# Two-layer recurrent trunk on one core: the second layer's embeddings placed between two matrix products, and a seven-product scheme on two more chunks

## The chip, the core and the metric

The kernel runs on one core of a Trainium2 chip. The core has a matrix engine (TensorE, PE in the profile, with PEld for the loading of its stationary operand), three engines for elementwise work (VectorE or DVE, ScalarE or ACT, GpSimd or POOL) and SyncE (SP), whose queue here only issues transfers. Each takes its instructions in the order that was fixed when the kernel was built, and waits on semaphores. The metric is the device time of one execution in microseconds.

## The reference

The reference computes, for 256 positions of width 2048, two layers of token mixers with residual adds, each followed by a gated per-layer embedding, and a last RMS norm. What matters here is the second layer (odd: `mlstm`) and the line of the embedding:

```
u = hn @ o_w_in[j]
qk, v, og, z, ig, fg = the columns of u (2048, 2048, 2048, 2048, 8, 8)
qk = jax.nn.silu(causal_conv(qk, c_conv_w[j], c_conv_b[j]))
...
yc = mlstm(q, k, v, li, lf)
yc = head_rmsnorm(yc, c_norm[j]) * jax.nn.sigmoid(og) * jax.nn.silu(z)
h = h + yc @ o_w_out[j]
pl = rmsnorm(p[i] @ ple_w[i], ple_norm[i])
h = h + jax.nn.sigmoid(h @ ple_gate_w[i]) * pl
```

The embedding `p[i] @ ple_w[i]` (256 x 256 by 256 x 2048) depends on nothing that the layer computes. All numbers are fp32.

## The kernel before

**Products in fp32.** Every fp32 operand is split into a rounded high part and a remainder (`hi`, `lo`), and a product is three matmuls: high by high, high by low, low by high. The weights are split as they arrive: `load_weights` (L124) takes a tile of 128 x 1024 (512 KB) into the ring `raw` (5 buffers), casts it on ScalarE into `whi` (L135) and subtracts on VectorE into `wlo` (L136), 4 buffers each. The activations, 256 positions by 2048 features, lie feature-major in `act`, eight entries of two blocks of 128 features each; they are TensorE's stationary operand, and the weights stream past in 512 columns.

**Chunks and quarters.** A weight matrix of 2048 columns is four chunks of 512; a chunk is four quarters of its 2048 rows. `quarter_tok` (L185) loads a quarter (two tiles) and issues 24 matmuls: 4 blocks of rows, two halves of the positions, three matmuls each. `project_tok` (L161) does a chunk; `project_two` (L170) does chunks 0 and 1 with their last quarters at the end, so that those features of the input that come late are wanted late; `chunks` (L180) is `project_two` and then chunks one by one. The two halves of a chunk are two accumulators in PSUM, from the pool `pm` (tag mm, 3 banks) or `px` (tag mx, 3 banks).

**Seven products.** `seven` (L262) does two chunks `j` and `j + 1` together. On their first quarter (256 features) it forms a 2 x 2 scheme over halves of the positions and the two chunks, with seven block products in place of eight: sums and differences of the weights on VectorE (`add`, L276), sums of the activations prepared once for all pairs (`combos`, L231, which gives `qs`), and combinations of the results in PSUM with the saved product `p1` (`soon`, L280; the copy of `p1`, L288). The other three quarters are plain (`plain`, L223, whose matmuls are at L217). It yields four results: chunk and half (0, 0), (0, 1), (1, 0), (1, 1). Its weights X and Y lie in tiles of tag ch (`chain`, 2 buffers), W and Z in the ring; the partial results in four half tiles from two tiles of tag h (`part`). The pool `hp` has four tiles of tag h; before this stage they hold the hidden state `hq`, which is sent away to DRAM (L1070) and fetched back (L1335). `combos` holds two scratch tiles of tag hn (3 buffers) through its three steps, and a third within each.

**Order.** The code is a list of instructions, and a scheduler puts each engine's share in order by its place in the list and by when its inputs are expected. `tc.high_priority(offset=n)` counts an instruction as if it stood n places earlier: 400 for weight casts and splits, 450 for `soon` and the copy of `p1`. Side work stands in lanes, generators that `pump` (L75) steps once in the middle of each quarter; `drain` steps a lane to its end. A lane often carries data from token-major to feature-major: two transposes on VectorE, one transfer to DRAM and four back on POOL's queue (`across`, L597), some pumps of lag, then scale, cast and split (L631, L149 and L150 for the gates; L492, L149 and L150 for the first layer's gate output, which makes `act` for the second layer).

**The second layer.** Its matrix products come in this order:
- queries and keys (`oqk`, L1126): four chunks by `chunks`; each is scaled to `tqk` and goes through `features` (L1096: hop across DRAM, convolution L1118, SiLU) in a lane;
- values (`ov`, L1267): four chunks, with the gate statistics and the mixing of the heads (`mix`) in lanes; `combos` starts after chunk 2;
- output gates (`oog`, L1308): two pairs by `seven`;
- z gates (`oz`, L1318): two pairs by `seven`; the result of chunk `j` is multiplied with the mixed heads and goes through lane `fm{j}` to `y`;
- the reload of the hidden state (L1335), then the embedding (`embed`, L411, called at L1345): two weight tiles' worth of chunks b, two halves c each, two halves of the positions, each a group of 6 matmuls (L438) in a bank of `pm` of its own, copied out to `pl` by ScalarE (L450, first half) or VectorE (L448, second half); in the first layer these copies have a preference of 600, here none;
- the output projection (`oo`, L1371): `chunks`, whose quarter kq waits for `y[2 kq]` and `y[2 kq + 1]`, that is for `fm{kq}`;
- the gate of the embedding and the last norm.

Of the kernel before, what the change touches and what calls it, by code (L numbers as in the profile page):

```python
# [19 lines left out]
P = 128  # L20
# [23 lines left out]
def trunk(ctx: ExitStack, tc: tile.TileContext, a, out):  # L44
# [37 lines left out]
    def drain(*which):  # L82
        for lane in which:
            while step(lane):
                pass
# [325 lines left out]
    def embed(w, pact, tile_of, first=None):  # L411

        pls = []
        for b in range(2):
            head = first and b == 0
            if head:
                part, pact = load_head(w[0])
                parts = [part] + load_weights(w[0], (1, 2), (1,))
            else:
                parts = load_weights(w[b], *(((2, 1),) if first else ()))  # L420
            if first and b:
                first()
            for c, (hi, lo) in enumerate(parts):
                terms = [(hf, k, x, y, 0, 512) for hf in range(2) for k in range(2) for x, y in ((0, 0), (0, 1), (1, 0))]
                if head:
                    terms.sort(key=(lambda t: (t[3], t[3] and t[0], t[1])) if c == 0 else
                               (lambda t: (t[1], t[3] if t[1] == 0 else t[0], t[3])))
                    if c == 0:
                        terms[0:4] = [(hf, 0, x, 0, o, T) for o in (0, T) for x in range(2) for hf in range(2)]
                pool, name = (px, "mx") if first and c == 0 else (pm, "mm")  # L430
                ps = [pool.tile([P, 512], F32, name=name, tag=name) for _ in range(2)]
                halves = []
                for n, (hf, k, x, y, o, w_) in enumerate(terms):
                    mine = [m for m, t in enumerate(terms) if t[0] == hf]
                    with ExitStack() as behind:
                        if first and "pe" in last:
                            behind.enter_context(tc.issue_after(last["pe"]))
                        last["pe"] = te.matmul(ps[hf][:, o:o + w_], tokens(pact[x], k, hf),  # L438
                                               (hi, lo)[y][:, k * 512 + o:k * 512 + o + w_],
                                               start=(n == mine[0]), stop=(n == mine[-1])).ins  # L440
                    if n < mine[-1]:
                        continue
                    pl = tile_of()
                    with ExitStack() as order:
                        if first:
                            order.enter_context(tc.high_priority(offset=600))
                        if hf and (b or not first):
                            v.tensor_copy(pl, ps[hf])  # L448
                        else:
                            s.copy(pl, ps[hf])  # L450
                    halves.append(pl)
                pls.append(halves)
        return pls
# [639 lines left out]
    with tc.tile_pool(name="m1", bufs=2) as m1:  # L1093
# [41 lines left out]
        VW = 258  # L1135
        vts = []
# [129 lines left out]
        qs = {}  # L1266
# [23 lines left out]
        turn = []  # L1290

        def part():
            n = len(turn) % 4
            turn.append(n)
            return store_of[n // 2][:, n % 2 * 512:(n % 2 + 1) * 512]

        def chain():
            return m1.tile([P, 1024], F32, name="ch", tag="ch", bufs=2)

        def pair(w, jj):  # L1300
            return seven(w, jj, acth, qs, chain, part)

        def mixed_gates():
            for j, th in [x for x in held if x[0] in nums]:
                v.scalar_tensor_tensor(nums[j], th, 1.0, nums[j], op0=ALU.add, op1=ALU.mult)
            held[:] = [x for x in held if x[0] not in nums]

        for jj in (0, 2):  # L1308
            ths = [m1.tile([P, 2, 512], F32, name="tho", tag="vt", bufs=6) for _ in range(2)]
            for b, hf, src in pair(a["oog"], jj):  # L1310
                s.activation(ths[b][:, hf], src, AF.Tanh, scale=norm["rth"][:, hf:hf + 1])
                if hf:
                    held.append((jj + b, ths[b]))
                    if jj + b == 3:
                        drain("mix")
                    mixed_gates()
        pact = load_p()
        for jj in (0, 2):  # L1318
            us = [m1.tile([P, 2, 512], F32, name="u", tag="vt", bufs=6) for _ in range(2)]
            for b, hf, src in pair(a["oz"], jj):  # L1320
                j, u = jj + b, us[b]
                with tc.high_priority(offset=100):
                    s.activation(u[:, hf], src, AF.Tanh, scale=norm["rth"][:, hf:hf + 1])
                    v.scalar_tensor_tensor(u[:, hf], u[:, hf], 1.0, src, op0=ALU.add, op1=ALU.mult)
                for i in range(2):
                    c = hf * 8 + 2 * j + i
                    e = slice(i * 256, (i + 1) * 256)
                    v.scalar_tensor_tensor(u[:, hf, e], u[:, hf, e], fac[:, c:c + 1], nums[j][:, hf, e],
                                           op0=ALU.mult, op1=ALU.mult)
                if hf:  # L1330
                    start(f"fm{j}", feature_major(u, "cn", 4 * j, y, 5))
# [3 lines left out]
            gp.dma_start(out=t, in_=away[c])  # L1335
            hq.append(t)

        pairs = []

        def pl_half():  # L1340
            n = len(pairs)
            pairs.append(pairs[n - 2] if n % 4 > 1 else m1.tile([P, 1024], F32, name="pl", tag="qk", bufs=4))
            return pairs[n][:, n % 4 // 2 * 512:(n % 4 // 2 + 1) * 512]
# [244 lines left out]
```

## Time and profile before

| | |
|---|---|
| median of 3 runs | 1034.44 us (1032.46 to 1036.43) |
| the profiled execution | 1034.75 us, span 1033.0 us |
| mean granted TensorE clock | 0.996 |
| DMA | 239.00 MB, mean 231 GB/s |

The span runs from the first to the last instruction of the profiled execution; the rest of its time lies around it. In the profile's rows by line, "mean ns of one" for matmuls is their modelled duration, and neighbours overlap; their pace is read from the distance of their starts. In rows of the timeline the first number is the start, the second the length, both in microseconds; what stands in brackets is the idle time of the engine just before and what ended it. In rows of stretches (start:end, length) the values are the busy time of PE, PEld, DVE, ACT and POOL with their instructions in parentheses, then the granted clock, the share of the DMA engines, and GB/s. In rows of the chain of waits: start, length, what.

The second layer's stages in this execution, from the same rows: queries and keys from about 475, values from about 563, output gates from 661.8, z gates to 833.6, the embedding from 833.62 to 849.67, then the output projection.

### The profile page before, as it was taken

The numbers are of one execution on the slowest core, as the hardware profiler recorded it, in microseconds if no ns is written. First come the engines' busy times: TensorE is split into PE (matmuls) and PEld (weight loads), VectorE is DVE, ScalarE is ACT, GpSimd is POOL, SyncE is SP. The second block draws the span as 40 slices with busy tenths as digits, with TensorE's granted clock in tenths as the row PEclk, the third lists the DMA queues.
The fourth block names the chain that finished last, engine by engine and source line by source line (L and its number), as shares of the span: only waits on it lengthen the run. The fifth ranks groups of instructions, "written<-read, shape, count | busy, mean of one in ns | idle before, by whom it ended". The sixth has DMA issues, their size and how long they took to land.

```text
span 1033.0 us, 14470 instructions
## 1 busy us (share of the span) xinstructions
PE 1020.5 (99%) x5206; PEld 847.1 (82%) x5206; DVE 786.8 (76%) x1194; ACT 615.8 (60%) x883; POOL 95.0 (9%) x178
## 2 busy tenths in 40 slices
PE   9999999999999999999999999999999989999996
PEld 8888888888888888887888888888888878888886
DVE  7858968969685776767569987887788886766684
ACT  7675545586964444565557876765565576344562
POOL 0111101011111111111021000000001111111000
PEclk9999999999999999999999999999999999999999
DMA  9987756567788897798797755464666787788652
GB/s 361 332 246 229 222 164 204 187 197 241 225 255 294 274 267 249 235 293 269 231 292 230 220 178 168 154 202 160 210 205 229 238 286 264 215 290 272 200 185 82
DMA packets 68808, 239.00 MB, mean 231 GB/s; under 512 B 8928, under 2 KB 10336, under 8 KB 68736
## 3 DMA queue, kind: packets, MB, share of 16 engines
q1 hardware_dynamic: 55584, 196.51, 58.4%
q0 software_dynamic: 12720, 41.04, 13.2%
q8 instruction: 41, 0.67, 0.3%
q10 hardware_dynamic: 432, 0.52, 0.1%
q14 instruction: 31, 0.25, 0.1%
HBM read 218.11 MB, written 19.92 MB: 230 GB/s over the span
## 4 chain that ended last, share of the span: by engine, by line
PE 93%; DMA 2%; issue 2%; ACT 1%; POOL 1%; DVE 0%; ACTq 0%; POOLq 0%
PE mm L196 21%; PE mm L197 21%; PE mm L198 21%; PE mm L217 9%; PE mx L196 4%; PE mx L197 4%; PE mx L198 4%; PE mx L217 3%; DMA r<-ducn 1%; PE mm L438 1%; PE nu L1241 1%; PE mm L1414 1%; PE mm L1413 1%; PE mm L1412 1%; DMA ducn<-w 1%
## 5 line engine op out<-in xcount | busy, mean ns | idle before, releaser
L136 DVE TENSOR_TENSOR wlo<-raw,whi 128x1024 fp32r<-128x1024 f32 (+1 forms) x341 | 411.8, 1215 | 168.3 <-ACT whi L135 158.6
L135 ACT CAST whi<-raw 128x1024 fp32r<-128x1024 f32 (+1 forms) x341 | 356.0, 1048 | 279.8 <-PE mm L198 184.0
L196 PE MATMUL mm<-whi,ahl 128*128 128x512 f32 x960 | 375.1, 391 | 0.0
L197 PE MATMUL mm<-wlo,ahl 128*128 128x512 f32 x960 | 373.9, 389 | 0.0
L198 PE MATMUL mm<-whi,ahl 128*128 128x512 f32 x960 | 373.6, 389 | 0.0
L196 PEld LDWEIGHTS mm<-whi,ahl 128*128 128x128 f32 x960 | 180.2, 188 | 38.2 <-issue 0.8
L198 PEld LDWEIGHTS mm<-whi,ahl 128*128 128x128 f32 x960 | 180.2, 188 | 37.7
L197 PEld LDWEIGHTS mm<-wlo,ahl 128*128 128x128 f32 x960 | 180.2, 188 | 37.0 <-DVE wlo L136 0.5
L217 PE MATMUL mm<-whi,ahl 128*128 128x512 f32 x320 | 101.2, 389 | 0.0
L217 PEld LDWEIGHTS mm<-whi,ahl 128*128 128x128 f32 x320 | 60.1, 188 | 12.4
L196 PE MATMUL mx<-whi,ahl 128*128 128x512 f32 x160 | 62.2, 389 | 0.0
L197 PE MATMUL mx<-wlo,ahl 128*128 128x512 f32 x160 | 62.2, 389 | 0.0
L198 PE MATMUL mx<-whi,ahl 128*128 128x512 f32 x160 | 62.2, 389 | 0.0
L217 PE MATMUL mm<-wlo,ahl 128*128 128x512 f32 x160 | 62.2, 389 | 0.0
L217 PE MATMUL mx<-whi,ahl 128*128 128x512 f32 x112 | 37.2, 390 | 0.0
L217 PEld LDWEIGHTS mm<-wlo,ahl 128*128 128x128 f32 x160 | 30.0, 188 | 6.3
L198 PEld LDWEIGHTS mx<-whi,ahl 128*128 128x128 f32 x160 | 30.0, 188 | 6.3
L196 PEld LDWEIGHTS mx<-whi,ahl 128*128 128x128 f32 x160 | 30.0, 188 | 6.2
L197 PEld LDWEIGHTS mx<-wlo,ahl 128*128 128x128 f32 x160 | 30.0, 188 | 6.2
L207 DVE TENSOR_TENSOR wlo<-ch,whi 128x1024 fp32r<-128x1024 f32 x20 | 24.1, 1222 | 9.6 <-ACT whi L206 8.9
L206 ACT CAST whi<-ch 128x1024 fp32r<-128x1024 f32 x20 | 21.0, 1051 | 13.1 <-PE mm L217 12.1
L217 PEld LDWEIGHTS mx<-whi,ahl 128*128 128x128 f32 x112 | 21.0, 188 | 4.3
(368 smaller groups left out, 1093.6 us busy)
## 6 DMA issues: line engine op xcount, KB each, us to landing
raw<-in_ew_dram SPq DMA_DIRECT2D x64, 512.0 KB, 5.0
raw<-in_g_dram SPq DMA_DIRECT2D x64, 512.0 KB, 4.9
raw<-in_eo_dram SPq DMA_DIRECT2D x32, 512.0 KB, 5.8
raw<-in_oqk_dram SPq DMA_DIRECT2D x32, 512.0 KB, 4.9
raw<-in_ov_dram SPq DMA_DIRECT2D x32, 512.0 KB, 4.2
raw<-in_oo_dram SPq DMA_DIRECT2D x32, 512.0 KB, 4.9
raw<-in_oog_dram SPq DMA_DIRECT2D x28, 512.0 KB, 4.1
raw<-in_oz_dram SPq DMA_DIRECT2D x28, 512.0 KB, 4.4
```

The source lines that it names most:

```text
L135: last["act"] = s.copy(h, r).ins
L136: last["dve"] = v.tensor_tensor(out=l, in0=r, in1=h.bitcast(F32), op=ALU.subtract).ins
L196: te.matmul(ps[hf], xh, wh, start=(k == 0), stop=False)
L197: te.matmul(ps[hf], xh, wl, start=False, stop=False)
L198: last["pe"] = te.matmul(ps[hf], xl, wh, start=False, stop=(k == KT - 1)).ins
L206: last["act"] = s.copy(hi, r).ins
L207: last["dve"] = v.tensor_tensor(out=lo, in0=r, in1=hi.bitcast(F32), op=ALU.subtract).ins
L217: last["pe"] = te.matmul(o, x, y, start=(first and k + i == 0), stop=(end and k == n - 1 and i == 2), skip_group_check=True).ins
L438: last["pe"] = te.matmul(ps[hf][:, o:o + w_], tokens(pact[x], k, hf), (hi, lo)[y][:, k * 512 + o:k * 512 + o + w_], start=(n == mine[0]), ...
L1241: te.matmul(ps[:, 0:n], x[:, i, o:o + P], y[:, b, i], start=(b == 0 and x is sh and y is vh), stop=(b == hf and y is vl))
L1412: te.matmul(o, xh, wh, start=(k == 0), stop=False)
L1413: te.matmul(o, xh, wl, start=False, stop=False)
```

## The change

Three things are changed.

1. The copies of the second layer's embedding out of PSUM get a preference of 450 instead of none.
2. Chunks 2 and 3 of the queries and keys are computed by `seven` instead of chunk by chunk. So `combos` starts before the queries and keys and steps in the pumps of their first quarters, and what `pair` needs (`part`, `chain`) is set up there; chunks 0 and 1 stay with `project_two`.
3. The embedding is called between the two pairs of z chunks instead of after both; its tiles and their loads from memory come with it.

```diff
@@ embed
-                        if first:
-                            order.enter_context(tc.high_priority(offset=600))
+                        order.enter_context(tc.high_priority(offset=600 if first else 450))
@@ queries and keys
-        for j, ps in enumerate(chunks(a["oqk"], 4, acth, ready(acth, "fg"))):
+        qs = {}
+        start("combos", combos(acth, 0, qs))
+        tqk = {}
+
+        def queries(j, hf, src):
+            if hf == 0:
+                tqk[j] = m1.tile([P, 2, 512], F32, name="tqk", tag="vt", bufs=6)
+            s.activation(tqk[j][:, hf], src, AF.Copy, scale=norm["rt"][:, hf:hf + 1])
+            if hf:
+                start(f"qk{j}", features(tqk[j], j))
+                step(f"qk{j}")
+
+        for j, ps in enumerate(project_two(a["oqk"], acth, ready(acth, "fg"))):
             if j == 0:
                 drain("norm")
-            t = m1.tile([P, 2, 512], F32, name="tqk", tag="vt", bufs=6)
             for hf in range(2):
-                s.activation(t[:, hf], ps[hf], AF.Copy, scale=norm["rt"][:, hf:hf + 1])
-            start(f"qk{j}", features(t, j))
-            step(f"qk{j}")
+                queries(j, hf, ps[hf])
+
+        drain("combos")
+        store_of = [hp.tile([P, 1024], F32, name="pr", tag="h") for _ in range(2)]
...
+        def pair(w, jj):
+            return seven(w, jj, acth, qs, chain, part)
+
+        for b, hf, src in pair(a["oqk"], 2):
+            queries(2 + b, hf, src)
@@ values
-            if j == 2:
-                start("combos", combos(acth, 0, qs))
...
-        drain("combos")
-        store_of = [hp.tile([P, 1024], F32, name="pr", tag="h") for _ in range(2)]
...
@@ z gates
         pact = load_p()
         for jj in (0, 2):
+            if jj:
+                pls = embed(a["pw1"], pact, pl_half)
             us = [m1.tile([P, 2, 512], F32, name="u", tag="vt", bufs=6) for _ in range(2)]
...
-        pls = embed(a["pw1"], pact, pl_half)
```

More of the change, by code (lines that the diff above doesn't have):

```diff
@@ L1124, in features, with part, chain @@
                 yield
-        for j, ps in enumerate(chunks(a["oqk"], 4, acth, ready(acth, "fg"))):
+        qs = {}
[9 more added lines that the diff above has]
+        for j, ps in enumerate(project_two(a["oqk"], acth, ready(acth, "fg"))):
             if j == 0:
                 drain("norm")
-            t = m1.tile([P, 2, 512], F32, name="tqk", tag="vt", bufs=6)
             for hf in range(2):
-                s.activation(t[:, hf], ps[hf], AF.Copy, scale=norm["rt"][:, hf:hf + 1])
-            start(f"qk{j}", features(t, j))
-            step(f"qk{j}")
+                queries(j, hf, ps[hf])
+        drain("combos")
+        store_of = [hp.tile([P, 1024], F32, name="pr", tag="h") for _ in range(2)]
+        turn = []
+        def part():
+            n = len(turn) % 4
+            turn.append(n)
+            return store_of[n // 2][:, n % 2 * 512:(n % 2 + 1) * 512]
+        def chain():
+            return m1.tile([P, 1024], F32, name="ch", tag="ch", bufs=2)
+        def pair(w, jj):
+            return seven(w, jj, acth, qs, chain, part)
+        for b, hf, src in pair(a["oqk"], 2):
+            queries(2 + b, hf, src)
         VW = 258
@@ L1264, in mix_norm @@
             yield
-        qs = {}
         for j in range(4):
@@ L1287, in trunk @@
         held = []
-        drain("combos")
-        store_of = [hp.tile([P, 1024], F32, name="pr", tag="h") for _ in range(2)]
[L1290 to L1301, printed above, removed]
         def mixed_gates():
@@ L1316, in trunk, with pl_half @@
                     mixed_gates()
+        pairs = []
+        def pl_half():
+            n = len(pairs)
+            pairs.append(pairs[n - 2] if n % 4 > 1 else m1.tile([P, 1024], F32, name="pl", tag="qk", bufs=4))
+            return pairs[n][:, n % 4 // 2 * 512:(n % 4 // 2 + 1) * 512]
         pact = load_p()
         for jj in (0, 2):
+            if jj:
+                pls = embed(a["pw1"], pact, pl_half)
             us = [m1.tile([P, 2, 512], F32, name="u", tag="vt", bufs=6) for _ in range(2)]
@@ L1336, in trunk @@
             hq.append(t)
[L1338 to L1343, printed above, removed]
-        pls = embed(a["pw1"], pact, pl_half)
         pss = m1.tile([P, 4, 2], F32, name="pss", bufs=1)
```

## The prediction

> **What bounds the kernel now.** I read the page's totals first, then TensorE's waits, then the chain of waits in order of time for TensorE's pace.
>
> ```profile
> span 1033.0 us, 14470 instructions
> PE 1020.5 (99%) x5206; PEld 847.1 (82%) x5206; DVE 786.8 (76%) x1194; ACT 615.8 (60%) x883; POOL 95.0 (9%) x178
> ...
> PE mm L438 <- ACT pl L450: 1.8, 1, 1.8
> PE mm L438 <- DVE pr L280: 1.2, 1, 1.2
> PE st L97 <- PEq L1579: 0.8, 1, 0.8
> PE mx L438 <- ACT whi L407: 0.3, 1, 0.3
> ...
> 510.53 1.00 PE mx L1062 x16
> ...
> 712.75 2.72 PE mx L217 x12
> ...
> 733.15 21.76 PE mm L217 x96
> 754.91 2.72 PE mx L217 x12
> ```
>
> TensorE is busy for 99% of the span. Between the start and the tail only two waits stand, both at L438 behind copies out of PSUM; they fall at 837 and 842, in the second layer's embed. So a saving must be fewer matmuls or a smoother embed; nothing else on TensorE can be won. The pace: 96 matmuls in 21.76 us are 0.227 us each (the "mean ns of one", 389, overlaps its neighbour). The two mx rows mark the same point of two neighbouring pairs: 42.16 us, which is 186 matmuls; two chunks the plain way (2 x 4 quarters x 24) are 192, or 43.5 us, 5.44 us a quarter.
>
> ```profile
> 833.62 0.39 PE L438 MATMUL mm<-whi,ahl 128*128 128x512 f32 x1
> ...
> 836.12 0.39 PE L438 MATMUL mm<-whi,ahl 128*128 128x512 f32 x1
> 836.36 0.57 ACT L450 COPY pl<-mm 128x512 f32<-128x512 f32 x1
> 836.87 0.68 DVE L280 TENSOR_TENSOR pr<-mm,pr 128x512 f32<-128x512 f32 x1
> ...
> 837.70 0.47 PE L438 MATMUL mm<-whi,ahl 128*128 128x512 f32 x1 [1.19 <-DVE pr L280]
> ...
> 840.09 0.51 ACT L631 ACTIVATE xr<-r,prm 128x256 f32<-128x256 f32 x1 [1.78 <-DMA r<-ducn]
> 840.31 0.39 PE L438 MATMUL mm<-whi,ahl 128*128 128x512 f32 x1
> ...
> 841.85 0.56 ACT L450 COPY pl<-mm 128x512 f32<-128x512 f32 x1
> ...
> 842.46 0.50 PE L438 MATMUL mm<-whi,ahl 128*128 128x512 f32 x1 [1.76 <-ACT pl L450]
> ...
> 849.67 0.39 PE L196 MATMUL mm<-whi,ahl 128*128 128x512 f32 x1
> ...
> 842.40:847.20 4.80, 4.74 (x14) 3.76 (x15) 3.85 (x7) 3.38 (x8) 0.00 (x0) 0.64 0.85 317
> ```
>
> The 48 matmuls of this embed run from 833.62 to 849.67, 16.05 us where 48 x 0.227 = 10.88 would do: 5.17 lost. From start to start less one matmul, the first gap is 837.70 - 836.12 - 0.23 = 1.35 (the third PSUM bank was still to be read by the pair's last combination, L280), the second 842.46 - 840.31 - 0.23 = 1.92. In the second, ScalarE had stood 1.78 us at the front of its queue for the hop of chunk 2's gates (r<-ducn) and took other work before the copy at 841.85. What remains, 5.17 - 1.35 - 1.92 = 1.90, is slow matmuls: in the last row the granted clock is 0.64 for 4.8 us, which alone is (1 - 0.64) x 4.8 = 1.7.
>
> **The change, part by part.**
>
> (1) Seven products for chunks 2 and 3 of queries and keys: 192 matmuls become 186, **-1.36 us** on the path. DMA stays at 16 tiles of 512 KB. Beside TensorE it adds three splits (19 for 16), four sums of weights, six combinations (24 of L280 in four pairs) and one copy:
>
> ```profile
> L136 DVE TENSOR_TENSOR wlo<-raw,whi 128x1024 fp32r<-128x1024 f32 x337 | 409.1, 1221 | 167.8 <-ACT whi L135 158.2
> L280 DVE TENSOR_TENSOR pr<-mm,pr 128x512 f32<-128x512 f32 x20 | 13.6, 682 | 0.0
> L276 DVE TENSOR_TENSOR ch<-ch,raw 128x1024 f32<-128x1024 f32 x8 | 9.8, 1222 | 0.1
> L135 ACT CAST whi<-raw 128x1024 fp32r<-128x1024 f32 x337 | 353.6, 1053 | 279.3 <-PE mm L198 184.0 <-PE mx L198 45.6 <-PE mm L217 15.8
> ...
> 519.70:563.20 43.50, 43.50 (x194) 36.02 (x193) 34.55 (x51) 27.97 (x41) 7.83 (x16) 1.00 0.86 266
> 563.20:606.70 43.50, 43.50 (x200) 36.18 (x199) 42.53 (x75) 32.97 (x52) 2.90 (x6) 1.00 0.70 215
> 606.70:661.80 55.10, 55.10 (x282) 47.16 (x281) 41.26 (x66) 38.54 (x83) 0.11 (x1) 1.00 0.46 148
> 791.60:833.60 42.00, 42.00 (x187) 34.78 (x186) 38.20 (x47) 26.73 (x35) 6.84 (x13) 1.00 0.77 251
> ```
>
> VectorE: 3 x 1.22 + 4 x 1.22 + 6 x 0.68 = 12.6 us; ScalarE: 3 x 1.05 + 0.57 (a copy as at 836.36) = 3.7. In the rows by stage the fourth value is VectorE's busy time. Chunks 2 and 3 ran from 519.7 to 563.2 with 34.55 of it; with 12.6 more it is 47.2 in 42.2, so 5.0 us too much, and the next stage (42.53 of 43.5) has 1.0 free. The rest must slip past 606.7, where 55.1 - 41.26 leaves 13.8, and the moved combos 4.9 more. What slips should be the convolutions and gate statistics, which have no preference, while splits and sums have 400 and combinations 450; the last gates' pair ran 38.20 of 42.0 without a TensorE wait. Cost on the path: from 0 (no TensorE wait stands there that could be won) to 5.0; I take 0.
>
> The first product needs a weight tile of tag ch at 519.7 (511.53, the end of L1062, plus 36 matmuls), the second 1.4 us later.
>
> ```profile
> 511.64 0.80 SPq L268 DMA_DIRECT2D ch<-in_oog_dram  x2
> ...
> DMA to landing us min/median/max: 4.2/4.9/7.0
> ```
>
> These loads, then for the next matrix, started just as L1062 ended. With the same start X lands at 515.8 to 518.6 and is split 2.3 us later, 518.1 to 520.9: 0 to 1.0 late; I take **+0.2**.
>
> (2) Combos, twelve VectorE and four ScalarE instructions, go from the values' stage to the first quarters of queries and keys. They hold all three buffers of tag hn (a21, a11 and the third), which the features of gate chunks 2 and 3 use too.
>
> ```profile
> L241 DVE TENSOR_TENSOR q<-xr,q 128x256 fp32r<-128x256 f32 x4 | 1.7, 418 | 0.5 <-ACT q L240 0.5
> ...
> 482.18 0.68 DVE L150 TENSOR_TENSOR ahl<-xr,ahl 128x512 fp32r<-128x512 f32 x1
> ```
>
> Twelve of about 0.41 are 4.9 us. The stage begins at 519.7 - 43.5 - 1.0 = 475.2 and wants chunk 2's features after two quarters, at 486.1; they were done at 482.9. If all 4.9 came first, 1.7 would be lost; if what is left of 3.2 us holds, nothing. I take 0: combos read only chunk 0, and can run before.
>
> (3) The embed moves between the two pairs of z, with its four weight loads on SP's queue, which now pass the second pair's; nothing of it is on POOL's. Its 48 matmuls stay. Copies get 450 instead of no preference, so they pass weight casts and splits.
>
> ```profile
> 792.58 0.68 DVE L280 TENSOR_TENSOR pr<-mm,pr 128x512 f32<-128x512 f32 x1
> ```
>
> At the new place the preceding pair's last combination ended at 793.3, 1.8 us after that pair's matmuls (833.62 - 42.16 = 791.5), where the third bank is wanted after 2.7. So the first gap should close; the second loses both causes, as no hop is due at that point (chunk 0's follows in program order, chunk 1's starts only then). Of 5.17 between nothing and all is saved; splits of 1.22 can still stand ahead of a copy, so I leave half the first gap, 0.7: **-4.5**.
>
> The price of a gap left over: this trace charged 1.90 for slow matmuls after its gap of 1.92 at 842.46, and next to nothing after that of 1.35, behind which 12 matmuls took 840.31 + 0.23 - 837.70 = 2.84 where 2.72 would do. So 0.7 gets no charge; with one it would be 1.9 more, a sum of -3.1 instead of the -5.0 below. The Trainium skill, "TensorE: Matmul & The Clock Gate", section "HAM oscillation — how this bites in real kernels", warns of idle gaps above about 3.4 us only, by which even 1.92 would have been free: this trace disagrees, with 0.64 granted after it. The Trainium skill, same page, section "A second HAM failure mode: psum-queue depth-cycling", says that short idles between groups that cycle PSUM banks can throttle too, which fits the row and speaks against any embed that still waits for its banks.
>
> (4) What the embed covered. It filled 16 us between the last gates and the output projection, while the features of chunks 2 and 3 crossed DRAM. Now the projection starts at the pair's end E (833.62 in this trace).
>
> ```profile
> 831.13 2.21 POOL L603 DMA_DIRECT2D r<-ducn  x4 [6.95 <-ACT whi L135]
> ...
> 842.31 0.62 ACT L149 CAST ahl<-xr 128x512 fp32r<-128x512 f32 x1
> ...
> 808.79 0.56 POOL L600 DMA_DIRECT2D ducn<-w  x1
> ...
> 850.33 0.54 POOL L600 DMA_DIRECT2D ducn<-w  x1 [10.20 <-DVE w L613]
> 850.53 0.67 DVE L150 TENSOR_TENSOR ahl<-xr,ahl 128x512 fp32r<-128x512 f32 x1
> ...
> 870.52 0.69 DVE L150 TENSOR_TENSOR ahl<-xr,ahl 128x512 fp32r<-128x512 f32 x1 [0.21 <-ACT ahl L149]
> ```
>
> Chunk 2's hop was back at 840.09, E + 6.5, its first cast done at E + 9.3; its remainder, 0.69 more, could be ready at E + 10.0. The third quarter wants it at E + 10.9 now (before: 16 us later). Slack is 0.9 where it was 17, and the remainder then ran only at 850.53, ready at E + 17.6, as nobody waited. So 0 to 6.7 us; near the ScalarE row, I take **+0.6**. Chunk 3's hop took 20.9 us from 850.33 to 871.2 and is wanted at E + 32.7 (seventh quarter), so it has to leave by E + 11.8. It stands behind two reloads of the hidden state on POOL, which wait for these gates. Chunk 1's, under a following pair, left at 808.79, 17.3 us after its matmuls; that would be 5.5 late. Plain quarters ask VectorE for 2 x 1.22 of 5.44 us only, so of 0 to 5.5 I take 0.
>
> Sum: -1.36 - 4.5 + 0.2 + 0.6 = -5.0. The profiled execution took 1034.75, span 1033.0 and 1.75 around it; it becomes 1029.7. The median is 0.3 lower, 1034.44: **1029.4**. With no residue the limit is 1034.44 - 1.36 - 5.17 = 1027.9.
>
> **Rivals.**
>
> *The third quarter of the output projection waits (slower).* With VectorE's order as in this trace, 6.7 us, and a clock charge as after 842 makes 8.6: 1027.9 + 8.6 = 1036.5. It speaks for it that 0.9 us is all the slack; against it, that these splits now come straight before matmuls that need them and VectorE has room in plain quarters. The time passes that of before when the wait with its charge exceeds 6.5, so from about 4.6 us. Its mild form, 2 us and a charge of 1.9, gives 1031.8. In all 14%.
>
> *The gaps travel with the embed.* The preceding pair, the copies and three banks are the same; if its last combination is again 3 us late and the clock drops, only 1.36 is won: 1033.1. Against it: the 792.58 row and the preference. 15%.
>
> *VectorE binds in the new pair.* If the 5.0 us fall on splits: 1027.9 + 5.0 = 1032.9, and 1034.8 with a clock charge. For it: 42.53 of 43.5 behind it; against it: no TensorE wait in that stage. 11%.
>
> **How the numbers follow.** The forecast has 60%, with 1027.9 to 1030.7. The range, 1027.6 to 1033.3, holds it (0.3 for spread below the limit), the second rival and about half of the others, some 85%. A measurement tells 0.5% from no change, that is 1029.3 and 1039.6: faster is 0.42 (most of the forecast's lower part), slower 0.03 (the first rival with a further wait), within 0.55.
>
> **What would show it.** 186 matmuls more at L217 for 192 fewer at L196 to L198, and no TensorE wait between the plain and the new pair; the 48 of L438 within 12 us at a clock of 1.00; matmuls without a gap 10.9 us into the output projection; convolutions (L1118) ending some microseconds later. Wrong would be gaps at L438 again, a wait on the second chunk's ahl, or one on wlo between 480 and 607.

## The result and the profile after

Timed in turn with the kernel before on one chip, the changed kernel takes 1040.89 us (six runs, 1039.68 to 1042.42) against 1034.22 (six runs, 1032.46 to 1036.43). The ratio is 1.0066, with a 95% interval of 1.0049 to 1.0082: **6.7 us slower**, where about 5 us faster was forecast. The profiled execution took 1041.62 us, its span 1039.8.

The totals of the profile after: span, then busy time, share and instructions of each engine.

```profile
span 1039.8 us, 14475 instructions
PE 1021.1 (98%) x5200; PEld 846.0 (81%) x5200; DVE 796.1 (77%) x1207; ACT 619.0 (60%) x887; POOL 94.9 (9%) x178
```

TensorE has six matmuls fewer and is busy as long as before (1021.1 us for 1020.5), so of the 6.8 us of span about 6 are time in which it stands. Its waits after, by what ended them (total us, times, longest):

```profile
PE mm L196 <- ACT whi L135: 3.0, 1, 3.0
PE mx L438 <- ACT whi L407: 1.3, 1, 1.3
PE mx L197 <- DVE wlo L136: 1.1, 1, 1.1
PE mx L1247 <- ACT khl L1240: 1.0, 1, 1.0
PE st L97 <- PEq L1588: 0.8, 1, 0.8
PE mm L197 <- DVE wlo L136: 0.8, 1, 0.8
PE mx L352 <- DVE s L347: 0.7, 1, 0.7
PE mx L1182 <- DVE gm L1178: 0.6, 1, 0.6
```

Both waits of the second layer's embed are gone (the L438 that is left, behind L407, is the first layer's, at the kernel's start). Six new ones stand in their place: three of 0.6 to 1.0 us on the gate statistics and heads (L1182, L352, L1247), which run beside the values, and three on split weights of the output projection (L196, L197). Line numbers after are one lower than before for the lanes, 9 higher at the end.

The stages between the first matmuls of each, from TensorE's timeline:

| stage | before, us | after, us | difference |
|---|---|---|---|
| to the first products | 15.93 | 17.32 | +1.39 |
| from there to chunk 2 of queries and keys | 503.87 | 503.60 | -0.27 |
| chunks 2 and 3 of queries and keys | 43.52 | 42.90 | -0.62 |
| values | 98.32 | 101.56 | +3.24 |
| output gates and z | 171.98 | 171.98 | 0.00 |
| embed | 16.05 | 10.88 | -5.17 |
| output projection to the end | 183.30 | 191.60 | +8.30 |
| span | 1032.97 | 1039.84 | +6.87 |

The output projection in the view by windows, before; then the embed, the output projection and a zoom into it, after (columns as in the prediction's rows of stretches):

```profile
849.67:1032.97 183.30, 174.88 (x817) 146.52 (x815) 122.52 (x198) 90.16 (x131) 15.92 (x29) 0.99 0.67 215
```

```profile
795.20:806.08 10.88, 10.88 (x49) 9.01 (x48) 10.88 (x15) 7.21 (x9) 0.12 (x1) 1.00 0.61 169
848.24:1039.80 191.56, 177.31 (x817) 147.47 (x815) 125.47 (x205) 92.92 (x138) 18.04 (x33) 0.97 0.67 215
929.00:934.00 5.00, 4.24 (x11) 3.17 (x12) 4.54 (x4) 2.72 (x3) 1.52 (x3) 0.66 0.86 211
```

The embed now runs at TensorE's pace, 48 matmuls in 10.88 us at a clock of 1.00. The output projection does the same 817 matmuls and needs 8.3 us more.

**What stops the output projection.** TensorE's rows around its longest gap, then ScalarE's (905 to 932 us), both after; the third fence is ScalarE before at the same work.

```profile
925.56 0.39 PE L198 MATMUL mm<-whi,ahl 128*128 128x512 f32 x1
928.93 0.50 PE L196 MATMUL mm<-whi,ahl 128*128 128x512 f32 x1 [2.98 <-ACT whi L135]
930.19 0.80 PE L197 MATMUL mm<-wlo,ahl 128*128 128x512 f32 x1 [0.76 <-DVE wlo L136]
```

```profile
915.42 1.05 ACT L135 CAST whi<-raw 128x1024 fp32r<-128x1024 f32 x1 [0.62 <-DVE ahl L501]
926.61 1.32 ACT L499 CAST ahl<-r 128x256 fp32r<-128x256 f32 x4 [10.14 <-DMA r<-dfo]
927.84 3.88 ACT L135 CAST whi<-raw 128x1024 fp32r<-128x1024 f32 x4
```

```profile
920.75 1.33 ACT L500 CAST ahl<-r 128x256 fp32r<-128x256 f32 x4 [4.54 <-DMA r<-dfo]
921.98 2.00 ACT L135 CAST whi<-raw 128x1024 fp32r<-128x1024 f32 x2
```

ScalarE did nothing for 10.14 us. At the head of its queue stood L499, the cast of the projection's own result coming back from DRAM for the next product. TensorE wants that only after the projection's 384 matmuls, so not before 848.24 + 4 x 21.76 = 935.3. Behind it stood four weight casts; they ran without a pause as soon as L499 was through, so their weights were there. TensorE lives on split weights, four tiles of whi, that is two quarters or 2 x 5.44 = 10.9 us of matmuls. They ran out: 928.93 - 925.56 - 0.23 = 3.14 us lost, then 930.19 - 928.93 - 0.23 = 1.03 until the first remainder, then about 1.7 at a clock of 0.66 ((1 - 0.66) x 5.0, the zoomed row). Before, the same idle time was 4.54 us and the stock bridged it. The Trainium skill, "Perfetto Trace Analysis", section "Tensor Engine Instruction (MATMUL, LD_WEIGHTS)", says that ScalarE's and VectorE's execution queues are strictly first in, first out; four casts that start only after L499 agree.

The hop itself, in rows of POOL's queue (start, time to issue, transfer; the bracket is POOL's wait, for the write to land in the last row), after and before; the first row after is chunk 3's gates on their way out:

```profile
855.75 0.54 POOL L599 DMA_DIRECT2D ducn<-w  x1 [2.62 <-DVE w L612]
...
902.36 1.10 POOL L467 DMA_DIRECT2D row<-in_rows_dram  x2
903.45 0.54 POOL L599 DMA_DIRECT2D dfo<-w  x1
919.88 2.22 POOL L602 DMA_DIRECT2D r<-dfo  x4 [15.89 <-DMA dfo<-w]
```

```profile
899.88 1.10 POOL L468 DMA_DIRECT2D row<-in_rows_dram  x2
900.97 0.54 POOL L600 DMA_DIRECT2D dfo<-w  x1
912.94 2.22 POOL L603 DMA_DIRECT2D r<-dfo  x4 [11.43 <-DMA dfo<-w]
```

The write stands behind two gain rows that are spread over 128 partitions, before and after. It took 4.5 us longer now, and left later in the stage (903.45 - 848.24 = 55.2 into it, before 900.97 - 849.67 = 51.3). A smaller gap of the same sort lies at 875.44 to 876.90 (1.23 us lost), where chunk 3's gates come back. ScalarE, VectorE and TensorE there, after:

```profile
871.49 1.31 ACT L630 ACTIVATE xr<-r,prm 128x256 f32<-128x256 f32 x3 [4.29 <-DMA r<-ducn]
...
873.22 1.05 ACT L135 CAST whi<-raw 128x1024 fp32r<-128x1024 f32 x1
```

```profile
873.81 1.29 DVE L1374 TENSOR_TENSOR pl<-pl,row 128x512 f32<-128x512 f32 x2 [6.74 <-DMA row<-in_rows_dram]
...
875.63 1.22 DVE L136 TENSOR_TENSOR wlo<-raw,whi 128x1024 fp32r<-128x1024 f32 x1
```

```profile
875.44 0.39 PE L196 MATMUL mx<-whi,ahl 128*128 128x512 f32 x1
876.90 0.50 PE L197 MATMUL mx<-wlo,ahl 128*128 128x512 f32 x1 [1.07 <-DVE wlo L136]
```

Here two queues stood still at once: ScalarE for the hop, VectorE for a gain row of the embedding's norm, which POOL issues only behind that hop (at 865.43, after the hop's reads at 863.23). The wait that ended last is VectorE's: the cast of the tile was done at 874.27, its remainder began only at 875.63, after the row's work and a split of features. The three gaps and the clock make 1.23 + 3.14 + 1.03 + 1.7 = 7.1 of the 8.3 us; another 1.1 lie behind the last matmul, from whose start to the end of the span it takes 9.77 us, before 8.70.

**What stops the values' stage.** VectorE's rows ahead of the first gate statistic that TensorE waits for at 574.01, and the stage's busy time up to the third wait:

```profile
571.59 0.69 DVE L1121 SCALAR_TENSOR_TENSOR qk<-th,qk 128x512 f32<-128x512 f32 x1
572.19 1.23 DVE L136 TENSOR_TENSOR wlo<-raw,whi 128x1024 fp32r<-128x1024 f32 x1
573.40 0.27 DVE L1175 MEMSET ae<- 64x256 f32 x1
573.60 0.36 DVE L1178 TENSOR_TENSOR gm<-mx,gm 128x256 fp32r<-128x256 f32 x1
```

```profile
563.82:610.10 46.28, 44.02 (x194) 35.45 (x192) 45.76 (x84) 35.23 (x57) 2.85 (x6) 1.00 0.71 220
```

No row has a bracket: VectorE never waits. It is busy for 45.76 of 46.28 us, and gm, which has no preference, comes when its turn comes. Before, VectorE was busy for 44.45 of the stage's first 46.28 us, and TensorE didn't wait: it had less than 2 us to spare. The matmul that needs gm stands in TensorE's order at a fixed place, with the values' matmuls behind it.

### The profile page after: what moved, and what is told of

The parts are those of the page before. It is cut to its first block, busy times and chain, and to the rows that moved or that the text cites. A ratio compares the mean times of both kernels' runs of the same rounds, so it can differ in the third digit from the quotient of the medians.

```text
span 1039.8 us, 14475 instructions
## 1 busy us (share of the span) xinstructions
PE 1021.1 (98%) x5200; PEld 846.0 (81%) x5200; DVE 796.1 (77%) x1207; ACT 619.0 (60%) x887; POOL 94.9 (9%) x178
## 5 line engine op out<-in xcount | busy, mean ns | idle before, releaser
L136 DVE TENSOR_TENSOR wlo<-raw,whi 128x1024 fp32r<-128x1024 f32 (+1 forms) x337 | 405.9, 1215 | 150.2 <-ACT whi L135 141.3
L135 ACT CAST whi<-raw 128x1024 fp32r<-128x1024 f32 (+1 forms) x337 | 350.8, 1047 | 261.7 <-PE mm L198 160.4
L196 PE MATMUL mm<-whi,ahl 128*128 128x512 f32 x896 | 350.7, 392 | 3.0 <-ACT whi L135 3.0
L197 PE MATMUL mm<-wlo,ahl 128*128 128x512 f32 x896 | 349.8, 390 | 0.8 <-DVE wlo L136 0.8
L198 PE MATMUL mm<-whi,ahl 128*128 128x512 f32 x896 | 349.2, 390 | 0.0
L196 PEld LDWEIGHTS mm<-whi,ahl 128*128 128x128 f32 x896 | 168.5, 188 | 39.2 <-ACT whi L135 3.4
L197 PEld LDWEIGHTS mm<-wlo,ahl 128*128 128x128 f32 x896 | 168.6, 188 | 35.3 <-DVE wlo L136 1.1
L198 PEld LDWEIGHTS mm<-whi,ahl 128*128 128x128 f32 x896 | 168.6, 188 | 35.2
L217 PE MATMUL mm<-whi,ahl 128*128 128x512 f32 x400 | 127.0, 389 | 0.0
L217 PEld LDWEIGHTS mm<-whi,ahl 128*128 128x128 f32 x400 | 75.1, 188 | 15.8 <-ACT pr L288 0.2
L217 PE MATMUL mm<-wlo,ahl 128*128 128x512 f32 x200 | 78.0, 390 | 0.1
L197 PE MATMUL mx<-wlo,ahl 128*128 128x512 f32 x160 | 62.4, 390 | 1.1 <-DVE wlo L136 1.1
L196 PE MATMUL mx<-whi,ahl 128*128 128x512 f32 x160 | 62.3, 389 | 0.0
L198 PE MATMUL mx<-whi,ahl 128*128 128x512 f32 x160 | 62.2, 389 | 0.0
L217 PE MATMUL mx<-whi,ahl 128*128 128x512 f32 x140 | 46.6, 390 | 0.0
L217 PEld LDWEIGHTS mm<-wlo,ahl 128*128 128x128 f32 x200 | 37.5, 188 | 8.4 <-DVE wlo L136 0.8
L207 DVE TENSOR_TENSOR wlo<-ch,whi 128x1024 fp32r<-128x1024 f32 x25 | 30.1, 1222 | 9.1 <-ACT whi L206 8.6
L197 PEld LDWEIGHTS mx<-wlo,ahl 128*128 128x128 f32 x160 | 30.0, 188 | 7.7 <-DVE wlo L136 1.5
L196 PEld LDWEIGHTS mx<-whi,ahl 128*128 128x128 f32 x160 | 30.0, 188 | 6.3
L198 PEld LDWEIGHTS mx<-whi,ahl 128*128 128x128 f32 x160 | 30.0, 188 | 6.2
L206 ACT CAST whi<-ch 128x1024 fp32r<-128x1024 f32 x25 | 26.4, 1055 | 13.6 <-PE mm L217 9.7
L217 PEld LDWEIGHTS mx<-whi,ahl 128*128 128x128 f32 x140 | 26.3, 188 | 5.4
```

What stands on the lines that cost most here:

```text
L135: last["act"] = s.copy(h, r).ins
L136: last["dve"] = v.tensor_tensor(out=l, in0=r, in1=h.bitcast(F32), op=ALU.subtract).ins
L196: te.matmul(ps[hf], xh, wh, start=(k == 0), stop=False)
L197: te.matmul(ps[hf], xh, wl, start=False, stop=False)
L198: last["pe"] = te.matmul(ps[hf], xl, wh, start=False, stop=(k == KT - 1)).ins
L206: last["act"] = s.copy(hi, r).ins
```

## The experiments

Three causes were put to the test: VectorE's extra work from the seven products, which surfaces at the statistics (against: the stage is disturbed by something that comes with the move); the gain rows ahead of the hops on POOL's queue; and the place of the hops' consumers at the head of ScalarE's queue, whatever delays the hop. The ratios are to the kernel before on the same chip in the same turns. Where an expectation uses a letter, it stands for the theory that it describes there.

**One part alone: the seven products.** The embed stays after both z pairs, its copies without preference.

```diff
-                        order.enter_context(tc.high_priority(offset=600 if first else 450))
+                        if first:
+                            order.enter_context(tc.high_priority(offset=600))
...
-            if jj:
-                pls = embed(a["pw1"], pact, pl_half)
...
+        pls = embed(a["pw1"], pact, pl_half)
```

> The seven products on the last two chunks of queries and keys alone; the embedding stays behind both z pairs, its copies without preference. Theory A (each edit has its own loss: the new pair wins 0.6 us, then the values' stage waits 3.1 us for VectorE and ScalarE, and the losses in the output projection belong to the move of the embedding): 2.5 us over before, about 1036.7; TensorE waits on gm, s and khl in the values' stage; none in the output projection; the embedding again 16 us. Theory B (all that was lost belongs to the move): about 1.4 us under before, 1032.8, no waits in the values' stage.

Measured: 1040.13 us, ratio 1.0057 (1.0038 to 1.0076). Three of TensorE's waits:

```profile
PE mx L1183 <- DVE gm L1179: 1.3, 1, 1.3
PE mx L1248 <- ACT khl L1241: 0.9, 1, 0.9
...
PE mx L352 <- DVE s L347: 0.7, 1, 0.7
```

The three waits beside the values come with this part alone; its values take 102.44 us where 98.32 were. In the output projection TensorE doesn't wait, and it takes 183.77 us to the end, as before. So the two losses belong to different parts of the change.

**One part alone: the move with its preference.** Queries and keys stay as before.

```diff
+                        order.enter_context(tc.high_priority(offset=600 if first else 450))
...
+            if jj:
+                pls = embed(a["pw1"], pact, pl_half)
...
-        pls = embed(a["pw1"], pact, pl_half)
```

> The embedding between the z pairs with preferred copies, without the new seven-product pair. Theory A: the embedding takes 10.9 us instead of 16 (5.2 won), and the output projection loses 1.5 us at the gain rows and about 6 us at a hop of its features, clock included: 2.3 us over before, about 1036.5. Theory B's rival, that the output projection's losses come from the changed order behind the seven products: 5.2 us under before, about 1029.0, no wait in the output projection.

Measured: 1035.41 us (1032.4 to 1040.4), ratio 1.0003 (0.9985 to 1.0021). The embed takes 10.88 us, so by the median what it wins is given back. The profiled execution is the fastest of the twelve; its output projection takes 185.02 us, 1.7 more than before. ScalarE there:

```profile
920.01 1.33 ACT L499 CAST ahl<-r 128x256 fp32r<-128x256 f32 x4 [7.91 <-DMA r<-dfo]
921.24 3.89 ACT L135 CAST whi<-raw 128x1024 fp32r<-128x1024 f32 x4
```

```profile
922.34 0.50 PE L196 MATMUL mm<-whi,ahl 128*128 128x512 f32 x1 [0.45 <-ACT whi L135]
```

The same place, a shorter idle time and a shorter gap: 7.91 us of ScalarE's cost TensorE a wait of 0.45, 10.14 cost 2.98 (both times 0.8 more follow at the first remainder), 4.54 cost none. Both costs leave 7.2 to 7.5 us that the stock of split weights bridges; what goes beyond falls on TensorE. Its executions spread over 8 us, so how late the hop comes may well vary from one to the next; no profile of a slower one shows it.

**One part alone: the preference.** Only the embed's copies get 450.

```diff
-                        if first:
-                            order.enter_context(tc.high_priority(offset=600))
+                        order.enter_context(tc.high_priority(offset=600 if first else 450))
```

> Only the preference of 450 for the embedding's copies, at its old place. Theory A (the second gap of 1.92 us and the slow clock of 1.9 us after it came from the copy's low place behind weight casts; the first gap of 1.35 us from the pair's last combination): 2 to 3.8 us under before, 1030.4 to 1032.2, one gap left at L438. Rival (ScalarE stands at the hop of the gates in any case, and the copy behind it): within 0.5 us of before.

Measured: 1033.85 us, ratio 0.9991 (0.9983 to 1.0000). The embed takes 12.76 us; the wait for the copy (pl) is gone, that for the pair's last combination (L280, 1.6 us) is not. The preference treats one gap of two, the place both. The theory had 2 to 3.8 us under before; it is about 0.9, since the wait for the copy is not always as long as in the profile before: without preference at the old place it was 1.8 us there, 0.2 in two of the kernels here and 3.6 in a third.

**The gain rows away from the hops.** The changed kernel, with the loads of the embedding's rows placed in the code ahead of the second z pair and those of the last norm after the output projection.

```diff
             us = [...]
+            if jj:
+                rows = row(m1, "vt", 6, 1)
...
-            fnr.extend(row(m1, "vt", 6, 2))
...
-            rows = row(m1, "vt", 6, 1)
...
         drain("emb")
+        fnr.extend(row(m1, "vt", 6, 2))
```

> The changed kernel with the gain rows of the embedding loaded right after it, in the second z pair, and the rows of the last norm loaded after the output projection, so that no broadcast row lies between the hops in POOL's queue. Theory A (rows arrive late and delay VectorE, and rows in the queue delay the second hop of the output projection): both waits of the output projection go, 7.5 us, about 1033.4. Rival (the hop is late by itself, since its own chunk and the transfers beside it are): the first wait of 1.5 us goes, the second stays, about 1039.4.

Measured: 1037.3 us, ratio 1.0021 (1.0003 to 1.0040): some 4.6 us better than the change (1.0066 - 1.0021), and still slower than before. The later gap is gone; the earlier one stays. VectorE no longer waits for a row there, but ScalarE does for the hop:

```profile
873.06 1.31 ACT L630 ACTIVATE xr<-r,prm 128x256 f32<-128x256 f32 x3 [6.87 <-DMA r<-ducn]
```

```profile
875.36 0.50 PE L196 MATMUL mx<-whi,ahl 128*128 128x512 f32 x1 [0.76 <-ACT whi L135]
```

```profile
852.12 0.53 POOL L467 DMA_DIRECT2D row<-in_rows_dram  x1
854.75 0.54 POOL L599 DMA_DIRECT2D ducn<-w  x1 [2.10 <-DVE w L612]
...
864.41 2.22 POOL L602 DMA_DIRECT2D r<-ducn  x4 [8.60 <-DMA ducn<-w]
```

Chunk 3's hop comes back later than in the changed kernel (873.06 - 847.24 = 25.8 us into the projection, there 23.3), and ScalarE, again at its consumer, idles for 6.87 us; 2.4 us are lost there in all. But the edit didn't take the rows away from this hop: POOL issued them only at 852.12 and 855.28, just before the hop's write and between the write and the reads, and the write took longer than in the changed kernel (8.60 us of POOL's wait for 6.94). So moving the rows moved the loss; what the earlier place would cost with no row near it, this run doesn't show. At the later place it does: without rows the write dfo<-w took 9.4 us where it took 15.9, ScalarE idled for 4.52 us, and TensorE didn't wait.

**The consumers later, the hops as they are.** The move with its preference, and more lag (in pumps) between a hop and its consumer: 6 for 5 for chunk 3's gates, 8 for 6 for the first two chunks of the output projection.

```diff
-        yield from across(w, r, f"d{name}{c}", 6)
+        yield from across(w, r, f"d{name}{c}", 8 if name == "fo" and c < 2 else 6)
...
-                    start(f"fm{j}", feature_major(u, "cn", 4 * j, y, 5))
+                    start(f"fm{j}", feature_major(u, "cn", 4 * j, y, 6 if j == 3 else 5))
```

> The embedding moved with preferred copies, no new pair, and two hops consumed later: the last z chunk's features one pump later (lag 6 for 5), those of chunks 0 and 1 of the output projection two pumps later (8 for 6); nothing else. Theory C (the output projection's waits are weight casts that stand behind a hop's cast in ScalarE's queue, a hop that the quarters there do not need yet): ScalarE's long idle times behind r<-dfo and r<-ducn go, no TensorE wait in the output projection, and the embedding's 5.2 us stay won: 1029 to 1031. Theory D (the transfers are slow, and the features are late for their own quarter): the wait stays or goes to the gate's second quarter, about 1035 as for the move alone.

Measured: 1031.40 us, ratio 0.9970 (0.9959 to 0.9981): faster than before. Its waits in the second layer:

```profile
PE mm L198 <- DVE ahl L150: 0.6, 1, 0.6
PE mx L197 <- DVE wlo L136: 0.4, 1, 0.4
```

No row was moved and no transfer made faster (POOL waits 13.53 us for the write dfo<-w); only the order on ScalarE and VectorE changed, and the gap behind r<-dfo is gone. That settles the cause of the later and larger loss. The earlier one isn't cured: the output projection still takes 185.26 us, 2.0 more than before. The wait of 0.6 at L198 (855.9 to 857.1, 10.9 us into the projection) is the third quarter's, which the prediction had priced at 0.6; with what follows it costs 0.9. The other 1.1 are lost between 873.5 and 876.2, at the wait for wlo. ScalarE stood only 0.89 us at chunk 3's hop there; VectorE stood for the gain row, with splits of weights behind:

```profile
871.40 1.30 DVE L1365 TENSOR_TENSOR pl<-pl,row 128x512 f32<-128x512 f32 x2 [6.55 <-DMA row<-in_rows_dram]
```

**The changed kernel with the same lags.**

> The changed kernel with the same two later consumptions. Theory C: the output projection's waits go (some 7 us of the profiled execution), what is left are the values' stage's waits (3.1 us): about 1033.5. Theory D: about 1040, as the change.

Measured: 1035.63 us, ratio 1.0001 (0.9985 to 1.0016). The hop's write was slow here too, and no longer matters:

```profile
920.43 2.21 POOL L602 DMA_DIRECT2D r<-dfo  x4 [14.20 <-DMA dfo<-w]
```

```profile
922.72 1.06 ACT L135 CAST whi<-raw 128x1024 fp32r<-128x1024 f32 x1 [0.31 <-PE mm L198]
923.68 1.32 ACT L499 CAST ahl<-r 128x256 fp32r<-128x256 f32 x4
```

L499 has no bracket: the weight casts run ahead of it, at TensorE's pace. ScalarE doesn't wait at chunk 3's hop either, and 1.0 us is still lost there, behind 6.62 us of VectorE's at the gain row, so what is left there is the row's. The waits beside the values stay (gm 1.3 and 0.3, khl 0.9, s 0.7). In the same turns the move with lags took 1031.40: with everything else repaired, the seven products cost 1035.63 - 1031.40 = 4.2 us, with six matmuls fewer.

**Less work for VectorE beside the values.** The seven products alone; of the 48 convolution sums (L1117 in the profile after) 32 are left out.

```diff
-                    for k in range(2, -1, -1):
+                    for k in range(2, 1, -1):
```

> The new seven-product pair alone, with the two older taps of the convolution of queries and keys left out (32 of 48 scaled sums of 0.47 us, 15 us of VectorE between 540 and 620). If the values' stage waits because VectorE's new 12.6 us push the gate statistics and the heads' inputs back, the TensorE waits on gm, s and khl go or shrink below 1 us in all. If they come from the order that was fixed for TensorE, they stay near 3 us.

Measured once: the waits on gm, s and khl are gone, and the values take 98.29 us, what they took before.

```profile
564.48:662.77 98.29, 98.29 (x479) 83.10 (x478) 74.58 (x113) 70.09 (x130) 2.97 (x7) 1.00 0.57 181
```

VectorE has 74.58 us there, where the seven products alone had 84.92. Its work is the cause, then. The time (1040.29) says nothing on it: the embed of this execution, at its old place, took 18.26 us.

**The statistics ahead of the convolutions.** The changed kernel with the lags, and the bodies of the gate statistics under a preference of 450.

```diff
-            v.memset(ae, 0.0)
-            gm = ...
+            with tc.high_priority(offset=450):
+                v.memset(ae, 0.0)
+                gm = ...
```

> The changed kernel with the two later hops and, besides, a preference of 450 for the gate statistics (as the combinations of the seven products have). Theory E (the values' stage waits because the gate statistics stand behind convolutions in VectorE's queue, pushed back by the new pair's 12.6 us): the TensorE waits on gm and s go, some 2.2 us, the one on khl stays: about 1033.4. Rival (VectorE is short in total there, so that something else is late instead): other waits of the same sum, about 1035.6.

Measured: 1036.45 us, ratio 1.0018 (1.0000 to 1.0037), no better than without it. The waits for gm and s are gone and the third has grown:

```profile
PE mx L1249 <- ACT khl L1242: 3.2, 1, 3.2
```

khl is cast from a convolved and gated chunk, so it waits for what was put behind. The stage takes 102.03 us. VectorE is short in total there; an order can only choose what is late.

**The move with lags, without preference.** The copies of the embed as before.

> The embedding moved with the two later hops, its copies without preference. If the place alone frees the embedding of its gaps (no hop is due there), it takes 10.9 us again and the time is that of the preferred one, about 1031.4. If the preference is needed at the new place, gaps at L438 come back with a slow clock behind them: 2 to 4 us more, 1033.5 to 1035.5.

Measured: 1031.81 us, ratio 0.9964 (0.9948 to 0.9981), not to be told from the one with it; the embed takes 10.90 us. The place alone closes both gaps. The one wait of its second layer, 1.3 us for wlo at L197, lies at the earlier place again; VectorE stood 7.61 us for the row, and 2.0 us are lost.

**The lags in the kernel before.**

> The kernel before with the two later hops alone. In its profiled execution TensorE did not wait in the output projection, though ScalarE stood 4.5 us at the same hop: within 0.5 us of before, 1034.6 to 1035.6, or up to 1 us under it if its slower executions are those in which that hop takes longer.

Measured: 1034.09 us, ratio 1.0003 (0.9987 to 1.0020). The lags win nothing by themselves, so the gain of the two kernels with the move comes from the move. The embed at its old place took 13.29 us here, not 16.05, and so did that of the seven products alone (13.30): the profile of before had caught a dear one. But the second z pair lost 1.5 us here (the gates and z together take 173.48 us, before 171.98): ScalarE stood 6.72 us at a hop of the gates (r<-ducn, to 827.83), and TensorE waited at L217 for split weights. The profile of before had 4.85 us of it at 825.08 and lost nothing. Every kernel with the move takes 171.99 us there, so against this one the move wins 13.29 + 173.48 - 10.88 - 171.99 = 3.9 us, of which the output projection takes back 2.0.

## Why the prediction was wrong

By its own steps:

- **(1) The seven products.** Six matmuls went (5200 for 5206), and the pair took 42.90 us, 0.62 less where 1.36 were hoped. The forecast's +0.2 was for a late X, but X and Y were in time (split by 519.7 and 521.3, their first products at 520.92 and 522.28). What came late, by 0.7 in steps from 524.21 to 526.82, is the plain quarter behind them: VectorE split its first weights only from 522.94 to 524.15, behind a transpose without preference and a sum of weights. The step that failed is *"Cost on the path: from 0 … to 5.0; I take 0"*. The prediction had counted 12.6 us more work for VectorE, seen 5.0 of it slip into a stage that is 42.53 of 43.5 us full, and let it fall on convolutions, which nobody on TensorE waits for at once. It came back as +3.2 us beside the values, within its 5.0. The slip did fall on work without preference, but that includes the statistics and the heads, whose small matmuls stand in TensorE's order between those of the values. The rival "VectorE binds in the new pair" had the engine right and the place mostly wrong: the one late split in the pair cost the 0.7 above.
- **(2) Combos.** No wait between 480 and 520; 0, as taken.
- **(3) The embed.** Both gaps closed and the clock stayed at 1.00: -5.17 in the profiles where -4.5 was taken. Right, and the preference wasn't needed. Right also that the gap left less than feared. What was off is the base: 16.05 us was one execution; in other kernels with the embed at that place it took 12.8 to 13.3 (once 18.3), so in the embed itself the move is worth some 2.4 us against those (13.3 - 10.9). What it saved besides, up to 1.6 us of waiting in the second z pair, the prediction didn't have; the profile of before shows none.
- **(4) What the embed covered.** The third quarter waited 0 in the changed kernel and 0.6 in the move with lags, as forecast. For chunk 3's hop, *"of 0 to 5.5 I take 0"* was argued from that hop's own quarter: it had to leave by E + 11.8. It left at 855.75 - 848.24 = E + 7.5, well in time, was back at E + 23.3, well before E + 32.7, and TensorE lost 1.2 us nonetheless: VectorE stood for the gain row that POOL issues behind this hop, with splits of other quarters behind, and of that loss 1.0 stayed when ScalarE no longer waited for the hop. The price of a late transfer isn't set by who needs its data but by **what is queued behind its consumer**. And the hops of the output projection (r<-dfo) have no term at all in the prediction. They aren't moved by the change, but all work around them shifted, and ScalarE waited 10.14 us for one of them with the casts of other quarters behind, which made the largest loss, 3.14 + 1.03 + 1.7 = 5.9 us. The profile of before had the row for it, 4.54 us of idle ScalarE at 920.75, and it wasn't read: with no wait on TensorE it looked free.

The first rival (the third quarter waits, with a clock charge) had the right stage and kind of loss and the wrong hop. The range ended at 1033.3 since the terms of 0 in (1) and for chunk 3's hop in (4), 3.2 and 1.2 us, were taken as independent small risks, and the 5.9 us of the projection's own hops had no term; all came. By medians the parts add up: 1.0057 for the seven products and 1.0003 for the move make 1.0060, measured 1.0066.

A part stays open. The seven products cost 4 to 6 us by median. By the profiles of the five kernels with them and all convolutions, 2.4 to 4.3 of it lie in the values' stage, less up to 1.0 in the pair. Another 0.4 to 1.1 lie behind the last matmul: from its start to the end, the kernels with the seven products take 9.1 to 9.8 us, all others 8.6 to 8.7. No run shows why; the rest isn't placed. The start of the kernel, which no variant touches, varied from 15.9 to 19.0 us over the profiled executions, so a single profile can't place it. Why the write dfo<-w took 15.9 us here and 11.4 before isn't settled either; rows ahead of it were there both times. And no run has the lags together with rows that are clear of chunk 3's hop, which would show whether the 1 to 2 us left at the earlier place can be won.

Of all versions the move with lags and without the seven products is fastest, 1031.4 us with the preference and 1031.8 without.

## What to carry to other kernels

Price a wait by what stands behind it in its engine's queue, not by who needs its result: an idle time of an engine that feeds TensorE is free only up to the stock it has laid in (in the output projection here some 7 us, by three profiles), so read the feeding engine's longest idle times even where TensorE shows no wait, before anything that covers them is moved. Where an engine is full over a stage, work added ahead of it comes out at whatever has no preference, and small matmuls in TensorE's fixed order count among that; an order of preference then only picks the victim.

## What the runs showed of the hardware

- The clock after a gap. In the changed kernel the gaps of 3.14 and 1.03 us were followed by a granted clock of 0.66 over 929 to 934; before, one of 1.92 us by 0.64. With the statistics preferred, TensorE stood 3.2 us for khl (to 611.24), and the clock stayed at 1.00:

```profile
607.40:612.40 5.00, 1.81 (x12) 1.23 (x10) 4.65 (x9) 1.88 (x3) 0.00 (x0) 1.00 0.65 202
```

  A gap's length alone doesn't decide, then. The Trainium skill, "TensorE: Matmul & The Clock Gate", section "What's actually happening", has the clock halved after an idle window of about 3.4 us; by that none of these gaps would be charged, and two were.
- A hop's time. Of the four writes of 512 KB in the output projection (dfo<-w, 128 partitions of 1024), the second, which POOL issues behind two gain rows, took 10.9 to 15.9 us from issue to landing over eleven kernels, the other three 5.2 to 8.7. With the rows taken away from it, in one kernel, the second took 9.4, still the longest of the four: the rows aren't all that makes it slow.
